# One engine per output tile, two engines in turn for the mixing, zeros in sixteen parts: a batched product of 8 x 12 heads on one core

## The chip, the cores and the metric

The kernel runs on one core of a Trainium2 chip. The metric is the device time of one execution in microseconds (us); the profiled span is about 1.8 us shorter than it (300.5 us of 302.28 in the profiled run of the kernel before). A ratio is the mean time of one kernel's fast runs over that of the other's fast runs of the same rounds, so it is not quite the ratio of the medians beside it.

Engine names in the profile: PE is TensorE (PEld its weight loads), DVE is VectorE, ACT is ScalarE, POOL is GpSimd, SP issues the DMAs. `L66` is a line of the kernel; L66 and L68 are the two branches of one copy helper, so groups are told apart by their tiles.

## The reference

```python
batch, n_heads, seq_t, seq_s, channels = 8, 12, 512, 512, 64
return np.einsum('bhtc,bhsc->bhts', x, y).astype(np.float32)
```

For each of 96 heads, x (512 x 64) times y transposed (64 x 512), all in float32. Inputs are 2 x 12.6 MB, the output is 100.7 MB: 125.8 MB have to cross between HBM and the core.

## The kernel before

x and y come in 12 groups of 8 heads into five buffers ("slots") of 2 MB each. A group is cast to bf16 (x to `xk`, y to `yb`), which frees its slot. `mix` spreads x into a zeroed buffer `xb`, VectorE transposes `xb` and `yb`, and TensorE makes each of 48 output tiles with eight matmuls in PSUM pieces of 3, 3 and 2 results of 128 x 512. The pieces are copied out ("evicted") into a slot, which one DMA stores. Loads and stores share the five slots.

```python
in_front = [nc.vector, nc.gpsimd, nc.vector, nc.scalar]
behind = [nc.vector, nc.gpsimd, nc.scalar, nc.vector]
FIRST = NG // 2          # 6
# ... (cut)
def mix(i, engines, halves=(0, 1)):      # four copies of 32 x 1024 into zeroed[i % 2]
    # ... (cut)
def result(o):
    i, h = divmod(o, 2)
    xT, yT = made[i]
    otf = slot()
    ot = otf.rearrange("p (r s) -> p r s", s=S)
    for k, n in ((0, 3), (3, 3), (6, 2)):
        pm = (pm3pool if n == 3 else pm2pool).tile([P, n, S], fp32, name=f"pm{n}")
        for j in range(n):
            nc.tensor.matmul(
                pm[:, j, :], xT[:, k + j, h, :], yT[:, h * S:(h + 1) * S], start=True, stop=True
            )
        copy(nc.scalar if n == 3 else nc.vector, ot[:, k:k + n, :], pm)
    if h == 0 and i + 2 < 2 * NG:
        transposes(i + 2)
    elif h == 1 and FIRST <= i + 4 < 2 * NG:
        mix(i + 4, behind)
    return lambda: nc.sync.dma_start(ov[i, h], otf)

with tc.manual_schedule():
    for g in range(SLOTS):
        load(g)
    nc.vector.memset(zeroed[0], 0.0)
    nc.gpsimd.memset(zeroed[1], 0.0)
    stores = []
    for g in range(NG):
        compress(g)
        mix(g // 2, [nc.gpsimd] * 4, (g % 2,))
        if g in (2, 4):
            transposes(g // 2 - 1)
        if g < 5:
            load(g + SLOTS)
        elif g in (5, 7, 9):
            stores.append(result(len(stores)))
        elif g in (6, 8):
            load(g // 2 + 7)
    for store in stores:
        store()
    for o in range(len(stores), 4 * NG):
        result(o)()
```

In the traces the engines work in program order: all 138 counted instructions of ScalarE before, 156 of VectorE and 54 of GpSimd (memsets and one table load left out) stand in the order in which the kernel issues them. The first three tiles are made between the last loads, and their stores are issued only after the last load (group 11).

## Time and profile before

301.96 us, median of three runs (301.9 to 302.25).

| | share of the span |
|---|---|
| the data queue on the 16 DMA engines | 98.7% |
| ScalarE busy | 66% |
| VectorE busy | 63% |
| TensorE busy | 49% |
| GpSimd busy | 27% |

Read the table from the top: one resource is full, and four have room. The prediction below shows the profile's lines for it. The page's list of DMA issues gives kilobytes and the median time from issue to landing (the moment when the transfer is reported done):

```profile
out_dram<-slot SPq DMA_DIRECT2D x48, 2048.0 KB, 21.7
```

The timeline of the issuing engine (start, duration, instruction) has the load of the last group:

```profile
53.29 0.33 SPq L75 DMA_DIRECT2D slot<-in_x_dram  x1
```

### The profile page before, as it was taken

To read this page: it belongs to the slowest core of one execution; us is meant where nothing else is said; L and a number is where in the kernel's file an instruction comes from. 1 tells how busy PE (TensorE), PEld (TensorE's weight loads), DVE (VectorE), ACT (ScalarE), POOL (GpSimd) and SP (SyncE) were. 2 spreads that over 40 slices of the span, in tenths; PEclk is the share of its full clock that TensorE was granted. 3 is DMA by queue.
4 is the path that set the end of the run, shared out by engine and by line. 5 is a ranking of instruction groups with operands and counts; after the bars stand their busy time and mean duration, and the time that the engine had idled before them with its cause. 6 is when DMAs were issued, how large, how long until landed. Compare 5 with 4: busy or idle time off the path is not lost.

```text
span 300.5 us, 1448 instructions
## 1 busy us (share of the span) xinstructions
PE 148.4 (49%) x384; PEld 47.6 (16%) x384; DVE 189.2 (63%) x157; ACT 198.1 (66%) x139; POOL 82.0 (27%) x59
## 2 busy tenths in 40 slices
PE   0004044228647573765675567666476767475000
PEld 0001011003212121221121122212121222121000
DVE  1568998895997669666767576757765775313000
ACT  4666598999976867686668676777677664647000
POOL 1899989991211011101110111011101100000000
PEclk9999575577997659567756855756955765955555
DMA  7999999999999999999999999999999999999994
GB/s 282 429 424 421 423 422 422 423 435 434 423 434 426 425 438 430 425 443 421 433 436 425 432 430 425 438 430 423 442 423 430 441 421 430 432 422 427 436 425 181
DMA packets 10377, 125.93 MB, mean 419 GB/s; under 512 B 1152, under 2 KB 1152, under 8 KB 1152
## 3 DMA queue, kind: packets, MB, share of 16 engines
q1 hardware_dynamic: 10368, 125.83, 98.7%
q8 instruction: 3, 0.05, 0.1%
q14 instruction: 6, 0.05, 0.0%
HBM read 25.17 MB, written 100.66 MB: 419 GB/s over the span
## 4 chain that ended last, share of the span: by engine, by line
DMA 65%; ACT 15%; DVE 7%; PE 3%; issue 1%; ACTq 1%; SPq 0%; DVEq 0%
DMA out_dram<-slot 56%; ACT slot L66 11%; DMA slot<-in_y_dram 9%; DVE yb L68 4%; PE pm L135 3%; ACT xk L83 3%; DVE xT L116 2%; ACT yb L66 2%; DVE slot L68 1%; DVE yT L121 1%; ACTq L191 0%; SPq L75 0%; ACTq L66 0%; DVEq L68 0%; SPq L143 0%
## 5 line engine op out<-in xcount | busy, mean ns | idle before, releaser
L135 PE MATMUL pm<-yT,xT 128*128 128x512 bf16 x384 | 148.4, 537 | 127.3 <-ACT slot L66 102.2
L66 ACT ACTIVATE slot<-pm 128x1536 f32<-128x1536 f32 x96 | 133.9, 1448 | 65.8 <-DMA out_dram<-slot 51.3
L68 DVE COPY slot<-pm 128x1024 f32<-128x1024 f32 x48 | 58.8, 1225 | 72.0 <-PE pm L135 54.4
L68 POOL COPY xb<-xk 32x1024 bf16<-32x1024 bf16 x42 | 62.2, 1482 | 145.4 <-DVE xT L116 144.3
L135 PEld LDWEIGHTS <-xT 128*128 128x128 bf16 x384 | 47.6, 124 | 227.2 <-issue 193.9
L116 DVE STREAM_TRANSPOSE xT<-xb 128x1024 uint32<-128x1024 uint32 x24 | 49.3, 2054 | 0.7
L68 DVE CAST yb<-slot 64x1024 bf16<-64x1024 f32 x24 | 35.2, 1466 | 13.5 <-DMA slot<-in_y_dram 13.2
L83 ACT ACTIVATE xk<-slot 128x2048 bf16<-128x2048 f32 x12 | 22.9, 1910 | 9.6 <-DMA slot<-in_x_dram 9.4
L68 DVE COPY xb<-xk 32x1024 bf16<-32x1024 bf16 x36 | 26.3, 731 | 0.5
L121 DVE STREAM_TRANSPOSE yT<-yb 128x512 uint32<-128x512 uint32 x24 | 25.0, 1041 | 0.0
L66 ACT ACTIVATE xb<-xk 32x1024 bf16<-32x1024 bf16 x18 | 24.1, 1338 | 0.4
L68 POOL CAST yb<-slot 64x1024 bf16<-64x1024 f32 x12 | 18.8, 1567 | 8.1 <-DMA slot<-in_y_dram 7.4
L66 ACT ACTIVATE yb<-slot 64x1024 bf16<-64x1024 f32 x12 | 15.9, 1324 | 3.6 <-DMA slot<-in_y_dram 3.4
L83 ACT ACT_TABLE_LOAD x1 | 1.3, 1283 | 0.7 <-PEq L180 0.7
L148 DVE MEMSET xb<- 128x1024 uint32 x1 | 0.9, 912 | 1.0 <-PEq L180 1.0
L149 POOL MEMSET xb<- 128x1024 uint32 x1 | 1.0, 952 | 0.3 <-POOLq L180 0.3
L180 POOL MEMSET const-float32-0.0<- 128x1 f32 x1 | 0.1, 98 | 0.2 <-issue 0.2
L180 POOL MEMSET const-float32-1.0<- 128x1 f32 x1 | 0.1, 98 | 0.0
L180 POOL MEMSET const-bfloat16-1.0<- 128x1 bf16 x1 | 0.1, 98 | 0.0
L180 POOL MEMSET const-uint8-127<- 128x1 uint8 x1 | 0.1, 98 | 0.0
## 6 DMA issues: line engine op xcount, KB each, us to landing
out_dram<-slot SPq DMA_DIRECT2D x48, 2048.0 KB, 21.7
slot<-in_x_dram SPq DMA_DIRECT2D x12, 1024.0 KB, 17.5
slot<-in_y_dram SPq DMA_DIRECT2D x12, 1024.0 KB, 19.3
```

The costliest lines, as they stand in the source:

```text
L66: nc.scalar.activation(dst, src, COPY)
L68: engine.tensor_copy(dst, src)
L83: nc.scalar.activation(xk.rearrange("p r c -> p (r c)"), both[:, :R * C], COPY)
L116: nc.vector.transpose(xT.rearrange("p (k r e) -> p k e r", k=K, e=E), xb.rearrange("p (k e c) -> p k e c", k=K, e=E),)
L121: nc.vector.transpose(yT.rearrange("p (r j) -> p j r", r=D), yb.rearrange("p (j c) -> p j c", c=D))
L135: nc.tensor.matmul(pm[:, j, :], xT[:, k + j, h, :], yT[:, h * S:(h + 1) * S], start=True, stop=True)
L148: nc.vector.memset(zeroed[0], 0.0)
L149: nc.gpsimd.memset(zeroed[1], 0.0)
L180: nc = _bacc.Bacc("TRN2", target_bir_lowering=False, num_devices=1)
```

## The change

The intent is to let a whole output tile leave PSUM by one engine, so that the other is free for other work meanwhile: three tiles in four by ScalarE, the fourth by VectorE. The mixing of x behind the loads goes to VectorE or ScalarE in turn and leaves GpSimd out: in the fourth tile, where VectorE evicts, ScalarE mixes. The zeroing of the two mixing buffers is cut into 16 memsets on each of two engines.

```diff
-    behind = [nc.vector, nc.gpsimd, nc.scalar, nc.vector]
...
-            copy(nc.scalar if n == 3 else nc.vector, ot[:, k:k + n, :], pm)
+            copy(nc.vector if o % 4 == 3 else nc.scalar, ot[:, k:k + n, :], pm)
         if h == 0 and i + 2 < 2 * NG:
             transposes(i + 2)
         elif h == 1 and FIRST <= i + 4 < 2 * NG:
-            mix(i + 4, behind)
+            mix(i + 4, [nc.scalar if o % 4 == 3 else nc.vector] * 4)
...
-        nc.vector.memset(zeroed[0], 0.0)
-        nc.gpsimd.memset(zeroed[1], 0.0)
+        for k in range(0, K * E * D, 64):
+            nc.vector.memset(zeroed[0][:, k:k + 64], 0.0)
+            nc.gpsimd.memset(zeroed[1][:, k:k + 64], 0.0)
```

## The prediction

Two passages are cut, where marked: the paragraph with the DMA's rate and two durations, and an allowance for another chip at the lower end of the range. Two durations are terms of the sums: 1.0 us for 1024 elements on ScalarE and 1.76 us for 1536 elements on VectorE. No trace from before the change shows them, so take them as the author's assumptions; the changed kernel measured 1.038 and 1.751 us. An estimate from the trace before, its copies of 1448 and 1225 ns scaled by the elements, gives 0.97 and 1.84 us. With the terms the sums came to 225 us for ScalarE, 188 for VectorE and 58 for GpSimd, and the forecast to 302.1 us in a range of 301.2 to 303.6; with the scaled ones ScalarE comes to 223.5 and VectorE to 190, and in the steady part four tiles take 16.6 and 14.0 us, still under the DMA's 19.5.

That the DMA has no more rate to give rests on its measured share alone: 1.01 at 430 GB/s from 100 to 240 us. That it moves as much beside a busy engine is in the trace: 429 GB/s from 80 to 90 us, with VectorE busy for 9.89 of 10 us, and 428 from 245 to 275 us, with VectorE busy for 10.37 of 30.

> **What bounds the kernel now.** I read the summary page first: the engines' shares, the slices with the DMA row, the queues.
>
> ```profile
> span 300.5 us, 1448 instructions
> ...
> PE 148.4 (49%) x384; PEld 47.6 (16%) x384; DVE 189.2 (63%) x157; ACT 198.1 (66%) x139; POOL 82.0 (27%) x59
> ...
> DMA  7999999999999999999999999999999999999994
> ...
> q1 hardware_dynamic: 10368, 125.83, 98.7%
> ...
> HBM read 25.17 MB, written 100.66 MB: 419 GB/s over the span
> ...
> DMA out_dram<-slot 56%; ACT slot L66 11%; DMA slot<-in_y_dram 9%; DVE yb L68 4%; PE pm L135 3%; ACT xk L83 3%; DVE xT L116 2%; ACT yb L66 2%; DVE slot L68 1%; DVE yT L121 1%; ACTq L191 0%; SPq L75 0%; ACTq L66 0%; DVEq L68 0%; SPq L143 0%
> ```
>
> No compute engine is above 66%, while the 16 DMA engines are at nine tenths or more in every slice but the first and the last, and the one data queue fills 98.7% of their span. The last line is the chain of waits: 65% of it is DMA, but 11% is ScalarE's eviction. That 11% needs a second look, because the change lengthens it. The busy-time windows and the chain in order of time show what it is:
>
> ```profile
> 100.00:240.00 140.00, 89.82 (x231) 28.60 (x229) 95.72 (x85) 98.80 (x72) 18.55 (x14) 0.67 1.01 430
> ```
> ```profile
> 152.17 2.80 ACT slot L66 x2
> 154.99 21.76 DMA out_dram<-slot
> ```
>
> Window columns are PE, weight loads, VectorE, ScalarE, GpSimd, granted clock, DMA share, GB/s. From 100 to 240 us the DMA share is 1.01 at 430 GB/s. A store is 100.66 MB / 48 = 2.097 MB, so it needs 2.097 / 0.430 = 4.88 us of all 16 engines. From issue to landing it takes 21.76 us, so about 17 us of that is queueing behind earlier stores. Eviction and landing together, 2.80 + 21.76 = 24.56 us, are five stores of 4.91 us: the loop of the five slot buffers turns at the DMA's pace. A longer eviction shortens the queueing, not the pace, as long as the queue stays filled. The waits confirm it:
>
> ```profile
> ACT slot L66 <- DMA out_dram<-slot: 51.3, 33, 2.7
> ```
>
> ScalarE waits 33 times, 51.3 us in all, for a store to free its slot.
>
> [...]
>
> **The change part by part.** These rows carry the durations:
>
> ```profile
> L66 ACT ACTIVATE slot<-pm 128x1536 f32<-128x1536 f32 x96 | 133.9, 1448 | 65.8 <-DMA out_dram<-slot 51.3
> L68 DVE COPY slot<-pm 128x1024 f32<-128x1024 f32 x48 | 58.8, 1225 | 72.0 <-PE pm L135 54.4
> L68 POOL COPY xb<-xk 32x1024 bf16<-32x1024 bf16 x42 | 62.2, 1482 | 145.4 <-DVE xT L116 144.3
> L68 DVE COPY xb<-xk 32x1024 bf16<-32x1024 bf16 x36 | 26.3, 731 | 0.5
> L66 ACT ACTIVATE xb<-xk 32x1024 bf16<-32x1024 bf16 x18 | 24.1, 1338 | 0.4
> ```
>
> *Evictions.* Before, each of 48 tiles took two ScalarE copies (133.9 / 48 = 2.79 us, they overlap a little) beside one VectorE copy of 1.225 us. After, 36 tiles take 2.79 + 1.0 = 3.8 us of ScalarE alone, and 12 take 2 x 1.76 + 1.225 = 4.7 us of VectorE alone. ScalarE: 36 x 3.8 = 137 against 133.9, +3 us. VectorE: 12 x 4.7 = 57 against 58.8, -2 us. The latency of one tile grows by 1.0 us (ScalarE) or 1.9 us (VectorE).
>
> *Mixing of x behind the loads.* There are 18 such steps of four copies. Before, each used one on GpSimd, one on ScalarE, two on VectorE. After, the nine with even index are all VectorE's (36 x 0.731 = 26.3 us, unchanged in sum) and the nine with odd index all ScalarE's (36 x 1.338 = 48.2 against 24.1, +24 us). GpSimd loses 18 copies of 1.3 us, -24 us. That GpSimd had 144 us of waiting in front of these copies shows that it was no bottleneck, so freeing it wins nothing.
>
> *Zeros.* Two memsets of 0.91 (VectorE) and 0.95 us (GpSimd) become 16 small ones each. The four tiny GpSimd memsets at the start read 0.10 us each, so 16 take at most about 1.6 us, an estimate: up to 0.7 us more. Both engines next work at 8.1 us, when the first y lands (VectorE sits idle 6.2 us before it), so all of it is hidden.
>
> *Sums.* ScalarE 198 + 3 + 24 = 225 us (75%), VectorE 189 - 2 + 1 = 188, GpSimd 82 - 24 = 58. In the steady part the unit is four tiles: the DMA needs 4 x 4.88 = 19.5 us. ScalarE: 3 x 3.8 + 4 x 1.338 = 16.8 us, 86% of that. VectorE: one eviction 4.7, two pairs of transposes 2 x (2.054 + 1.041), four copies 2.9: 13.8 us, 71%. Both fit beside the DMA; the gain and the cost on the path that sets the end are both about 0.
>
> *Where the slack is thinnest.* Before the stores start, the queue holds only loads, and each waits until ScalarE, VectorE and GpSimd have read the slot before it. The last load (x and y of group 11) is issued at 53.3 us. Counted in bytes, (53.3 - 2.9) us x 423 GB/s = 21.3 MB of the 23.1 MB issued have moved, so some 4 us of queue are left. ScalarE's order before that issue now contains two extra 1024-element copies (tiles 0 and 1), about 2.0 us, of which 0.9 fall into ScalarE's idle time before tile 1 (it waited 0.92 us there for a VectorE cast, and VectorE now has one copy less). So the load slips by about 1.1 us and some 2.9 us of queue are left. A DMA on an empty queue took about 2 us to full rate at the start (issued at 0.74, 418 GB/s from 3 us). Margin: under 1 us, but positive.
>
> **The rivals.** (1) The slot loop lengthens: if the 21.7 us of landing were a latency and not queueing, each of some nine turns of the chain would grow by 1.0 to 1.9 us, for 311 to 319 us. For it speaks only the 11% of ScalarE in the chain; against it the DMA share of 1.01 and 17 us of queueing. (2) ScalarE becomes the bound. If its mix and VectorE's eviction did not overlap, four tiles would take 16.8 + 4.7 = 21.5 us against 19.5, +2 us in each of ten rounds: about 320 us. For it: each engine is in order, and the ScalarE mix may not overwrite its buffer before VectorE has transposed the earlier contents. Against it: that transpose is issued one tile earlier, ahead of VectorE's own eviction, and the queue of 17 us absorbs a late round. (3) A gap in the DMA at 54 to 70 us: if the slip of the last load is 2 us more than estimated, or the first VectorE tile (tile 3, after the casts of group 11) comes late, the loss is once, 1 to 3 us: 303 to 305 us. (4) A gain: even perfect overlap has only the first 3 us and the last 4 us, when the DMA is part idle, to win, and no part of the change touches either: the last store left ScalarE and VectorE about 22 us before the end. The final tile is now VectorE's and about 2 us later, still inside that.
>
> **Range and chances.** The centre is the time before, 301.96, plus a few hundredths for rival 3 in small: 302.1 us. The three runs before span 0.35 us; with a small gap of up to 1.5 us upwards[...], the range is 301.2 to 303.6. Over 2% slower means beyond 308, which only rivals 1 and 2 reach: 2%. Over 2% faster means under 296, which would need more than the DMA's rate allows: 1%.
>
> **What would show it right or wrong.** Right: the DMA row still reads 9 in all inner slices; 98% or more for the queue; ScalarE near 225 us, VectorE near 188, GpSimd near 58; the 1024-element ScalarE copy near 1.0 us and the 1536-element VectorE copy near 1.76; median landing of a store about 1 us shorter than 21.7, the pace the same; ScalarE's wait for stores shrunk. Wrong: a slice with the DMA at 8 or less between 50 and 100 us (rival 3), ScalarE above 90% and waiting for transposes with the DMA row below 9 through the second half (rival 2), or unchanged landing times with longer loops (rival 1).

## The result, and the profile after

302.14 us, median of six runs (302.1 to 302.28), against 302.29 us for the kernel before in the same rounds (301.9 to 302.38). The ratio is 0.9999, 95% interval 0.9986 to 1.0012: the same.

From the page of the changed kernel:

```profile
span 300.3 us, 1412 instructions
...
PE 145.4 (48%) x377; PEld 46.5 (15%) x384; DVE 182.6 (61%) x160; ACT 221.3 (74%) x169; POOL 59.1 (20%) x56
...
DMA  7999999999999999999999999999999999999994
...
q1 hardware_dynamic: 10368, 125.83, 98.8%
...
DMA out_dram<-slot 53%; ACT slot L66 8%; DVE slot L68 7%; ACT xb L66 2%; ACT xk L83 1%; DVEq L192 1%; PE pm L135 0%; ACT yb L66 0%; DVE yb L68 0%; DVEq L68 0%; ACTq L66 0%
...
out_dram<-slot SPq DMA_DIRECT2D x48, 2048.0 KB, 20.6
```

ScalarE worked 23.2 us more and GpSimd 22.9 us less, and the span moved by 0.2 us. The DMA row is digit for digit what it was. The landing of a store became 1.1 us shorter: this is where the longer eviction went. In the timelines a tile's eviction grew by 0.92 us for three tiles in four (2.79 to 3.71) and by 1.76 us for the fourth (2.79 to 4.55), 1.13 us in the mean. The window from 100 to 240 us (engines in the order of the prediction's window line) has the same 430 GB/s:

```profile
100.00:240.00 140.00, 87.38 (x222) 27.73 (x226) 92.74 (x79) 116.86 (x93) 0.00 (x0) 0.70 1.01 430
```

The groups of instructions, with shapes kept apart, give the durations that the prediction had to assume (busy us, mean ns of one, then idle time before them):

```profile
L66 ACT ACTIVATE slot<-pm 128x1536 f32<-128x1536 f32 x72 | 100.8, 1453 | 37.9 <-DMA out_dram<-slot 27.7 <-PE pm L135 5.1 <-DVE yb L68 2.6
...
L66 ACT ACTIVATE xb<-xk 32x1024 bf16<-32x1024 bf16 x36 | 48.2, 1338 | 0.8
...
L68 DVE COPY slot<-pm 128x1536 f32<-128x1536 f32 x24 | 41.0, 1751 | 72.5 <-DMA out_dram<-slot 38.0 <-PE pm L135 34.5
...
L66 ACT ACTIVATE slot<-pm 128x1024 f32<-128x1024 f32 x36 | 37.4, 1038 | 0.0
```

ScalarE's 51.3 us of waiting for stores became 27.7: it still waits for the DMA, only less. VectorE's waiting for stores rose from 15.8 to 38.0 us, because it now writes whole tiles; the two together went from 67.1 to 65.7 us. And the last load is issued about one microsecond later than before (53.29 us there):

```profile
54.33 0.33 SPq L75 DMA_DIRECT2D slot<-in_x_dram  x1
```

### The profile page after: what moved, and what is told of

It reads as the page before. It is cut to its first block, busy times and chain, and to the rows that moved or that the text cites. A ratio compares the mean times of both kernels' runs of the same rounds, so it can differ in the third digit from the quotient of the medians.

```text
span 300.3 us, 1412 instructions
## 1 busy us (share of the span) xinstructions
PE 145.4 (48%) x377; PEld 46.5 (15%) x384; DVE 182.6 (61%) x160; ACT 221.3 (74%) x169; POOL 59.1 (20%) x56
## 4 chain that ended last, share of the span: by engine, by line
DMA 53%; ACT 11%; DVE 7%; issue 1%; DVEq 1%; PE 0%; ACTq 0%
DMA out_dram<-slot 53%; ACT slot L66 8%; DVE slot L68 7%; ACT xb L66 2%; ACT xk L83 1%; DVEq L192 1%; PE pm L135 0%; ACT yb L66 0%; DVE yb L68 0%; DVEq L68 0%; ACTq L66 0%
## 5 line engine op out<-in xcount | busy, mean ns | idle before, releaser
L135 PE MATMUL pm<-yT,xT 128*128 128x512 bf16 x377 | 145.4, 524 | 129.7 <-ACT slot L66 74.3
L66 ACT ACTIVATE slot<-pm 128x1536 f32<-128x1536 f32 (+1 forms) x108 | 133.2, 1314 | 37.9 <-DMA out_dram<-slot 27.7
L68 DVE COPY slot<-pm 128x1536 f32<-128x1536 f32 (+1 forms) x36 | 54.6, 1571 | 72.5 <-DMA out_dram<-slot 38.0
L135 PEld LDWEIGHTS <-xT 128*128 128x128 bf16 x384 | 46.5, 121 | 227.7 <-issue 194.0
L66 ACT ACTIVATE xb<-xk 32x1024 bf16<-32x1024 bf16 x36 | 48.2, 1338 | 0.8
L68 DVE CAST yb<-slot 64x1024 bf16<-64x1024 f32 x24 | 33.8, 1408 | 17.6 <-DMA slot<-in_y_dram 17.3
L68 POOL COPY xb<-xk 32x1024 bf16<-32x1024 bf16 x24 | 38.5, 1606 | 1.2
L83 ACT ACTIVATE xk<-slot 128x2048 bf16<-128x2048 f32 x12 | 22.9, 1910 | 9.6 <-DMA slot<-in_x_dram 9.5
L149 DVE MEMSET xb<- 128x64 uint32 x16 | 1.2, 112 | 0.8 <-PEq L181 0.8
L150 POOL MEMSET xb<- 128x64 uint32 x16 | 1.4, 151 | 0.3 <-POOLq L181 0.3
## 6 DMA issues: line engine op xcount, KB each, us to landing
out_dram<-slot SPq DMA_DIRECT2D x48, 2048.0 KB, 20.6
```

What stands on the lines that cost most here:

```text
L66: nc.scalar.activation(dst, src, COPY)
L68: engine.tensor_copy(dst, src)
L83: nc.scalar.activation(xk.rearrange("p r c -> p (r c)"), both[:, :R * C], COPY)
L135: nc.tensor.matmul(pm[:, j, :], xT[:, k + j, h, :], yT[:, h * S:(h + 1) * S], start=True, stop=True)
L149: nc.vector.memset(zeroed[0][:, k:k + 64], 0.0)
L150: nc.gpsimd.memset(zeroed[1][:, k:k + 64], 0.0)
```

## The experiments

The theory: the DMA engines set the time, and the stores queued behind five slots absorb what the change costs the engines. Two rivals predict the same 302 us: that costs and gains of the parts cancel, and that the change costs the engines nothing. The experiments take the parts apart, take the DMA's bound away, and take the slack away.

### Each part alone

Edits to the kernel before, each a part of the diff above: the new eviction line alone, the new mixing line alone, the small memsets alone.

> The kernel before with the new evictions alone (a whole tile by one engine). Theory (the DMA engines set the time, the slot queue hides the longer eviction): 302 us, within 0.3% of before, landing of a store about 1 us shorter than 21.7. Rival (two effects cancel: longer evictions cost, freeing GpSimd gains): slower, 305 to 312 us.

> The kernel before with the new mixing alone (VectorE and ScalarE in turn, no GpSimd). Theory: 302 us, within 0.3% of before, although ScalarE gains 24 us of work. Rival (two effects cancel): faster, 292 to 299 us.

> The kernel before with the 32 small memsets alone. Both theories: 302 us; VectorE and GpSimd still wait for the first y until 8.1 us.

| | median us | ratio to before (95%) | ScalarE busy us | median landing us |
|---|---|---|---|---|
| evictions alone | 302.27 | 0.9996 (0.9981 to 1.0011) | 197.8 | 20.6 |
| mixing alone | 302.44 | 1.0004 (0.9989 to 1.0019) | 222.1 | 19.6 |
| zeros alone (one round) | 302.06 | 0.9991 (0.9971 to 1.0011) | 198.0 | 21.7 |

(Before, in the same rounds: 302.29 us.) No part gains or loses more than the noise, so at full stores nothing of size cancels. The eviction alone shortens the landing by 1.1 us. The mixing alone adds 24 us of ScalarE work for 0.04%, and it too shortens the median landing, by 2.1 us: the queue absorbs this too, though no eviction became longer. The late issue of the last load belongs to the evictions: it is at 54.27 us with them alone and at 53.11 us with the mixing alone.

### Half the bytes stored: the engines become the bound

Only the first half of each row group is stored, from the kernel before, from the changed one, and from each of the two larger parts. The output is wrong (half of it stays unwritten); the work of the engines is complete.

```diff
-        return lambda: nc.sync.dma_start(ov[i, h], otf)
+        return lambda: nc.sync.dma_start(ov[i, h][:, :, :K * S // 2], otf[:, :K * S // 2])
```

> The kernel before, storing only the first half of each output row group (wrong on purpose: half of the output stays unwritten). The DMA's floor falls to 75.5 MB / 430 GB/s + 7 = 183 us. Theory: now the engines set the pace after 66 us, at the 3.45 us per tile that the trace showed between 66 and 83 us: about 222 us. Rival (a latency of the store binds, not its bytes): far less of a fall, 270 us or more.

> The changed kernel, storing only half as well (wrong on purpose). Theory: the cost of the change was hidden by the DMA and now shows: about 4.1 us per tile after 66 us, ScalarE the bound, about 246 us, 9 to 12% slower than before with half stores. Rival (the change costs the engines nothing): equal to before with half stores.

> Before with the new evictions alone, half stores (wrong on purpose). Per four tiles ScalarE has 3 x 3.71 + 2 x 1.34 = 13.8 us, VectorE 4.55 + 6.2 + 2.9 = 13.7 us, hardly other than before (13.8 and 14.0). Theory: within 4% of before with half stores. Rival (one engine per tile is what costs): 8% or more slower.

> Before with the new mixing alone, half stores (wrong on purpose). Per four tiles ScalarE has 4 x 2.79 + 4 x 1.34 = 16.5 us against 13.8. Theory: this part is what costs, 8 to 12% slower than before with half stores, near the changed kernel's time. Rival: within 3% of it.

| half stores | median us | over before with half stores |
|---|---|---|
| before | 222.07 | |
| changed | 249.14 | +12.2% |
| evictions alone | 234.21 | +5.5% |
| mixing alone | 263.34 | +18.6% |

(The last column divides the medians; the four ran together on one chip.) Windows from 90 to 180 us of before, changed, evictions alone and mixing alone, all with half stores; the figures after the duration are PE, PEld, DVE, ACT, POOL, granted TensorE clock (as a share of full speed), DMA share, GB/s:

```profile
90.00:180.00 90.00, 56.82 (x212) 21.11 (x211) 88.42 (x80) 89.08 (x66) 17.33 (x13) 0.96 0.74 305
```
```profile
90.00:180.00 90.00, 58.05 (x181) 19.44 (x180) 70.91 (x59) 89.34 (x73) 0.00 (x0) 0.84 0.63 260
```
```profile
90.00:180.00 90.00, 59.91 (x197) 20.85 (x197) 84.09 (x69) 83.87 (x69) 16.12 (x13) 0.89 0.69 283
```
```profile
90.00:180.00 90.00, 50.07 (x160) 17.75 (x159) 66.44 (x60) 80.93 (x60) 0.00 (x0) 0.78 0.57 233
```

The DMA share falls below 0.75 and the engines fill up. The kernel before came out at the 222 us expected, so the rival that a latency of the store binds (270 us or more) falls. Before, VectorE (88.42) and ScalarE (89.08) are both full: the work was well balanced. In the changed kernel ScalarE is full (89.34) and VectorE is at 70.91 of 90 us, so ScalarE is the bound. So the rival that the change costs the engines nothing falls: where the engines bind, it costs 27 us (246 us were expected, 249.14 measured), and with full stores the DMA hides this.

The two parts missed what was expected of them. Evictions alone were to be within 4% and cost 5.5%. Their busy time is as counted, but both engines are only 93% busy, and in this window ScalarE stands 5.7 us and VectorE 5.1 us waiting for TensorE, against 0.2 and 0.3 us in the kernel before. Whether the order of the pieces or TensorE's lower granted clock (0.89 against 0.96) makes these waits, no run tells. Mixing alone was to cost 8 to 12% and costs 18.6%, though neither ScalarE nor VectorE is full in its window; the two together cost less than mixing alone. The count of busy time could not tell this, the order on the engines can. (Here too the clock is lower, 0.78, but TensorE is busy for only 50.07 of 90 us.) Timeline of mixing alone, one eviction round (start, duration, instruction, idle time before it and what ended it):

```profile
100.81 5.43 ACT L66 ACTIVATE xb<-xk 32x1024 bf16<-32x1024 bf16 x4 [1.40 <-DVE xT L116]
...
106.26 2.79 ACT L66 ACTIVATE slot<-pm 128x1536 f32<-128x1536 f32 x2
...
107.76 7.31 PE L135 MATMUL pm<-yT,xT 128*128 128x512 bf16 x19 [4.43 <-ACT slot L66]
...
111.49 1.23 DVE L68 COPY slot<-pm 128x1024 f32<-128x1024 f32 x1 [4.11 <-ACT slot L66]
```

While ScalarE mixes for 5.43 us it evicts nothing, and the two larger pieces of every tile are its own to evict. TensorE stands 4.43 us, and VectorE, whose piece of the tile comes third, then waits 4.11 us for one. Over this whole run and over before with half stores, the waits say:

```profile
DVE slot L68 <- ACT slot L66: 40.8, 12, 4.1
```
```profile
DVE slot L68 <- ACT slot L66: 4.0, 3, 1.5
```

In the changed kernel with half stores VectorE evicts a whole tile beside ScalarE's mixing:

```profile
111.45 4.55 DVE L68 COPY slot<-pm 128x1536 f32<-128x1536 f32 x3 [1.40 <-PE pm L135]
...
112.83 5.44 ACT L66 ACTIVATE xb<-xk 32x1024 bf16<-32x1024 bf16 x4
```

So the two parts belong together: given the mixing in turn, the new evictions win 14.2 us back (263.34 to 249.14). Against the kernel before, which spreads the mixing over three engines, the pair still loses while the engines bind.

### The slack at the last load

Tile 1 is evicted twice (the same values), so that ScalarE frees the slot of the last load later.

```diff
-            copy(nc.vector if o % 4 == 3 else nc.scalar, ot[:, k:k + n, :], pm)
+            for _ in range(2 if o == 1 else 1):
+                copy(nc.vector if o % 4 == 3 else nc.scalar, ot[:, k:k + n, :], pm)
```

> The changed kernel with tile 1 evicted twice by ScalarE (the same values), so that the last load is issued 3.7 us later, at about 58.0 us instead of 54.3. Theory with the thin margin of the prediction (2.9 us of queue left, about 2 us to refill an empty queue): the queue runs dry at about 57.4 us, the DMA row shows a hole near 57 to 60 us, and the time grows by 2 to 3.5 us to 304 to 305.5 us. Rival (the slack there is larger than counted): 302 us, no hole.

Measured: 305.99 us, ratio to before 1.0119 (1.0102 to 1.0136). The load is issued at 58.45 us. Windows of one microsecond, the last two figures the DMA share and GB/s:

```profile
56.00:57.00 1.00, 0.12 (x1) 0.00 (x0) 1.00 (x1) 0.99 (x1) 0.94 (x2) 0.50 1.02 426
57.00:58.00 1.00, 0.00 (x0) 0.00 (x0) 1.00 (x2) 0.98 (x1) 1.00 (x1) 0.50 0.05 16
58.00:59.00 1.00, 0.00 (x0) 0.00 (x0) 1.00 (x2) 0.98 (x2) 0.94 (x2) 0.50 0.00 0
59.00:60.00 1.00, 0.00 (x0) 0.00 (x0) 1.00 (x1) 1.00 (x1) 0.94 (x2) 0.50 0.36 74
60.00:61.00 1.00, 0.00 (x0) 0.00 (x0) 0.99 (x2) 0.97 (x2) 1.00 (x1) 0.50 0.81 319
61.00:62.00 1.00, 0.00 (x0) 0.00 (x0) 0.79 (x1) 0.92 (x2) 0.96 (x2) 0.50 0.99 418
```

The queue runs dry just after 57 us. Windows of half a microsecond show 164 GB/s from 60.0 to 60.5 us and 475 from 60.5 to 61.0, so the full rate is back 2.0 us after the issue (the 2.5 us that the expectation of the ring of two below takes from this run was read from the one-microsecond windows). The thin margin is real, and it can be sized roughly: the load slipped by 58.45 - 54.33 = 4.12 us against the changed kernel, and the time grew by 305.99 - 302.14 = 3.85 us, so by the time about 0.3 us of slip was free (the two medians are of two measuring sessions, with the kernel before at 302.29 us in both). That is a little more growth than the 2 to 3.5 us expected. The shares missing from 57 to 61 us add up to only 2.8 us, which would leave 1.3 us free; the rest of the growth fits the stretch from 63 to 66 us, where the windows show 319, 221 and 246 GB/s at a share near 1. What slowed the transfers there is open, and so the margin is known only as 0.3 to 1.3 us.

### Fewer slots

Three runs were meant to leave only two or three slots in turn from tile 10 on, by asking for the others and not using them.

```diff
         otf = slot()
+        if o >= 10 and o % 2 == 1:
+            for _ in range(SLOTS - 2):
+                slot()
```

In the first of their expectations the time that a store takes beyond its 4.9 us of transfer is cut, where marked: no run had shown it by then. With it a store came to 6.9 us, and all three expectations count with that; the ring of two below measured a landing of 6.9 us.

> The kernel before, with only two of the five output slots in turn from tile 10 on, the stores unchanged. A loop of two is one eviction of 2.8 us plus a store of 4.9 us[...]: (2.8 + 6.9) / 2 = 4.9 us per tile, just at the DMA's pace. Theory: 302 to 312 us.

> The changed kernel with two slots in turn from tile 10 on. Theory (queueing was what hid the longer eviction; with almost none left it shows): evictions of 3.7 (three in four) and 4.55 us give about 5.4 us per tile, 12 to 25 us slower than before with two slots. Rival (the longer eviction is harmless whatever the queue): equal to before with two slots.

> The changed kernel with three slots in turn from tile 10 on: (3.7 to 4.55 + 6.9) / 3 = 3.6 us per tile, under the DMA's 4.88. Theory: still 302 to 304 us, with landing times near 3 x 4.9 - 3.9 = 10.8 us instead of 20.6. Rival (a latency binds): 320 us or more.

They measured 302.05, 301.98 and 302.18 us with landings of 21.7, 20.6 and 20.6 us, the same as with five. The reason, from the buffer addresses of the built programs: an unused buffer is given back at once, and the stores kept rotating through all five. The unchanged landings agree. These runs tested nothing, and that two of the times lie in the expected ranges counts for nothing. The mended edit keeps two buffers and writes them in turn:

```diff
-        otf = slot()
+        if 10 <= o < 10 + 2:
+            ring.append(slot())
+        otf = slot() if o < 10 else ring[o % 2]
```

Here too a term beside the 4.9 us of transfer is cut. With it a landing came to 7.4 to 8.4 us, of which only the lower end is read from a run (the one with the late load).

> The changed kernel with the same two output buffers used in turn from tile 10 on (the three runs with two or three slots kept rotating through five buffers, so they tested nothing). At most one store is then queued behind the one that runs. A loop of two is two tiles: one eviction of 3.7 us (4.55 for one tile in four) and one landing of an almost unqueued store, 4.9 us of transfer[...] (2.5 us to refill an empty queue was seen with the late load). Theory (the queue behind five slots hides the eviction; without it each tile pays): (3.9 + 7.4 to 8.4) / 2 = 5.7 to 6.2 us per tile instead of 4.88, for 38 tiles: 330 to 350 us, landing 7 to 9 us, DMA row below 9. Rival (eviction is harmless whatever the queue): 302 us.

Measured: 326.50 us, ratio to before 1.0798 (1.078 to 1.0816). The first line is the landing of all 48 stores, the second the window of before:

```profile
DMA to landing us min/median/max: 6.6/6.9/20.9
```
```profile
100.00:240.00 140.00, 72.06 (x182) 22.49 (x181) 75.15 (x65) 92.40 (x74) 0.00 (x0) 0.67 0.90 381
```

The landing falls from 20.6 to 6.9 us without a faster store, so some 14 us of it were queueing. From tile 10 on the evicting engine waits 35 times for a store to land (25 times in the changed kernel with five slots). With little queue left, the DMA share falls to 0.90, and the loop of two costs (326.50 - 302.14) / 38 = 0.64 us a tile. The estimate from the measured landing, (3.9 + 6.9) / 2 = 5.4 us instead of 4.88, gives 0.52 of these; the remaining 0.12 us is not accounted for (the chain of waits of this run also passes through VectorE's transposes and mixing, from 159.37 to 166.98 us for one). The range expected (330 to 350 us) was too high because it took 7.4 to 8.4 us for the landing; measured is 6.9, 2.0 more than the 4.88 us of a store at 430 GB/s. No run of the kernel before with a ring of two was made, so how much the longer eviction alone would cost there is not shown. Shown is that, with at most one store queued, the time grows; that the eviction is the part of the loop that shows is argued from the sum above. Shown with the long queue is that a longer eviction is hidden.

No version that beats both was tried: 125.8 MB at the 430 GB/s of the full windows take 293 us of a span of 300, and the rest is the first 3 us and the last 4.

## Why the prediction was right

**The bound.** The step that carried it was that the eviction on the chain of waits is part of a loop that turns at the DMA's pace, and that a longer eviction shortens the queueing. The landing went from 21.7 to 20.6 us at the same 430 GB/s, with the evictions alone just as with the whole change; this side is shown. With two buffers the landing fell to 6.9 us and the time grew, as the step says for a queue that does not stay filled; there the eviction's own share is argued, not measured.

**The sums.** The assumed copies measured 1.038 us (1.0 assumed) and 1.751 us (1.76). ScalarE came to 221.3 us (225), GpSimd to 59.1 (58). VectorE came to 182.6 us against 188, the largest miss: its evictions fill 54.6 us of time instead of 57, because consecutive copies overlap (4.55 us a tile instead of 4.7), and the casts of y take 33.8 instead of 35.2 us. Neither is on the path that sets the end.

**The zeros.** 16 memsets took 1.22 us on VectorE and 1.37 us on GpSimd; both still waited for y until 8.1 us. Hidden, as said.

**The thinnest slack.** A slip of 1.1 us was predicted, 1.04 measured. The margin was called under 1 us but positive; the late load puts it between 0.3 and 1.3 us. The two figures behind it held: about 2.7 us of queue were left at the issue (2.9 predicted, the queue dry just after 57 us) and the refill took 2.0 us (2 predicted). The prediction was right here with little to spare, and with some luck: the margin, 2.7 - 2.0 = 0.7 us by the measured figures, is a small difference of two rough ones.

**The rivals.** A store latency as bound (rival 1) falls by the landing times; ScalarE as bound (rival 2) is real only with half stores, where its cost shows as 27 us. The overlap that the prediction set against rival 2, VectorE's eviction beside ScalarE's mixing, is in the trace. What it did not see is how much hangs on it: mixing alone, without that overlap, costs 41 us with half stores. The one-time gap (rival 3) did not open, and the gain (rival 4) did not come.

## What to carry to other kernels

In this kernel the DMA engines were full in every slice but the first and the last, and an engine's share of the chain of waits was no lever: 11% of the chain before was ScalarE's eviction, and a tile's eviction longer by 0.92 us for three tiles in four moved nothing, as the landing shrank from 21.7 to 20.6 us. So see first whether the landing time of the transfer beside it in the chain is mostly queueing. This kernel hid both losses and gains of its engines: the change costs 27 us with half stores and nothing measurable with full ones (ratio 0.9999), and the new evictions, given the mixing in turn, win 14.2 us with half stores and 0.3 us with full ones (302.44 to 302.14, within the noise). So judge an engine-side change of such a kernel with the transfers cut down, and look for the one place where the queue is thin. Which engine takes which piece should be decided together: an engine with a long block of other work should not owe a piece of every tile in that time (in the round shown, 5.43 us of mixing on ScalarE, behind which TensorE stood for 4.43 us and VectorE waited for 4.11).
